# Value products of two batches in one visit, and projection products tilted over eight steps, in a hybrid attention block

## The chip, the cores and the metric

The kernel runs on one core of one Trainium2 chip. Its time is the device time of one execution in microseconds (us); for a kernel with several runs the median is given. Stage times come from one profiled execution.

## The reference, cut to what matters

One layer of an encoder block over 1024 tokens of width 1024, in float32:

```python
h = x @ w_in                       # 3328 columns
q_a, k_a, v_a, z_a, q_b, k_b, v_b, z_b = split(h)
y_a = neighborhood_attention(q_a, k_a, v_a, rel_bias)   # 8 heads of 64, grid 16 x 64, window 8 x 16
y_b = windowed_gqa_with_sink(rotary(q_b), rotary(k_b), v_b, sink)   # 8 query heads, 2 kv heads, |i - j| <= 128
mixed = concat(y_a * silu(z_a), y_b * silu(z_b))
x = layer_norm(alpha * x + mixed @ w_out)
```

Both attentions take a softmax over their scores: `softmax(q k^T / 8 + bias)` in the neighbourhood group (a), and with one more logit for each head, the sink, in the windowed group (b).

## The kernel before, in words

Float32 products are made of float16 parts: each operand is split into a high and a low half, and three products (high x high, low x high, high x low) are summed in PSUM.

**Stages.** A first stage makes the values v of all tokens and the first six of 21 projections (`project`, names in `ORDER`, 48 products of 512 columns each: two halves of 24). The middle stage, which the change touches, runs the attention in *steps*, one for each *unit*. The last stage multiplies by w_out, adds the residual and normalises.

**Units, batches and quads.** A unit is one head's softmax for 128 queries. There are 128: 64 of group b, then 64 of group a. Four units in a row form a *batch* for the scores and a *quad* q for the values; quad q is units 4q to 4q+3, and its scores are batch q. Quads 0 to 15 are of group b, 16 to 31 of group a.

**What happens to a unit.** The scores of a batch go to four of five PSUM banks named `s` (`batch`, `stage_mm`, L933). DVE adds the bias and takes the row's extreme (`stage_qk`, L958, tiles `sn` and `nm`), ACT takes the exponential and its sum (`stage_exp`, L974), DVE the reciprocal of the sums of two units (`stage_sum`, L980 and L981, tile `ri`). Then `stage_tr` splits the probabilities into halves (ACT L992, DVE L993, tile `split`), which empties the bank, and SP issues a transposing DMA to tile `tr` (L999), of which three quads' worth exist. The value products of a quad (`stage_pv`, L1035) read `tr` and the values (`vb` or, gathered by `gather_v`, `va`) and write one half of the only bank `t`: even quads the first half, odd quads the second. `stage_z` (L1043 and L1046, DVE) multiplies that half into the gate tile `z`, which frees it.

**Steps.** In the loop over steps i, every fourth step (i = 3, 7, 11, ...) issues the scores of the next batch, and behind them the value products that `PV_AT` has for this step: quad q at step 4q + 11, with the last two at 131 and 135. `Z_AT` gives the step of the z product, mostly 4q + 13.

**Projections as filling.** The other 15 projections and the first products with w_out (60 of them, L1165) run between these on TensorE. They form the list `fill`; `pump_to(u)` issues as many of them as are due by the time u, which may lie within a step. `FILL_AT` has the steps at which each projection begins, `WARP` bends the time within four steps. A finished half of a projection is taken out of its PSUM bank `pj` (two banks) by `evac`: by ACT and DVE, for rotary ones by POOL too. Such operations wait in queues of the program for each engine (`enq`), from which `pop(engine, n, top)` emits those that are due at fixed places of a step; `top` = 0 takes only the urgent ones, such as the emptying of a `pj` bank. `need` emits one at once, where something depends on it.

**Order.** The order of each engine's instructions is the order of emission, fixed when the program is built. Nothing overtakes on an engine or in SP's queue of DMA issues.

Of the kernel before, what the change touches and what calls it, by code (L numbers as in the profile page):

```python
# [25 lines left out]
QSCALE = 2.0 ** -15  # L26
BH, BR, NX, F1 = 6, 6, 6, 0.2
NSPLIT, NP = 6, 2
ORDER = ["zb0", "z0", "zb1", "kb", "qb0", "z1", "qb1", "zb2", "qb2", "k0", "qb3", "q0", "zb3", "k1", "q1",
         "k2", "q2", "k3", "q3", "z2", "z3"]  # L30
NPRO = 6
NS = 21 - NPRO
ZPRO = (0, 1, 2, 5)
ZSUM = (1, 6, 13, 14)
DSUM = (4, 7)
SUMS = list(range(11)) + [13, 11, 14, 12]
NR = 8
# [1 line left out]
SCALE_AT = ((4, 6), (7, 2))  # L39
K_ORDER = (5, 0, 6, 1, 7, 2, 3, 4)  # L40
FILL = ORDER[NPRO:]
FILL_AT = [0, 8, 17, 25, 33, 41, 49, 57, 65.5, 74, 82, 90, 98, 106, 113.5, 122.5, 125, 127, 128.5, 131.5, 136]
ZTAG = {"z3": "zv", "zb3": "zc", "z2": "zs", "zb1": "zd", "zb2": "ze"}
X2POOL = (1, 3, 5)
WVPOOL = (3, 5)
# [5 lines left out]
WO_PRE = (9, 10, 12, 13, 14, 15)  # L51
WO_POST = (7, 8)
WO_MAX = 88
EO = (4, 5, 6, 7, 0, 1, 2, 3)
LAST = ((0, 384), (384, 128))
NPE = 384
# [18 lines left out]
def hybrid_block(ctx, tc, xT, x, wt, wv, wo, bias, sink, gain, lbias, cos, sin, bmask, out):  # L75
# [45 lines left out]
    invt = const.tile([128, 2], F32, name="invt")  # L121
    NT = len(ORDER)
    xsc = const.tile([128, 1], F32, name="xsc")
# [56 lines left out]
    def pop(eng, n, top=1, late=0):  # L180
        q = queues[eng]
        ready = [op for op in q if op.prio <= top and all(
            d.step is not None and d.step + d.lag < clock["step"] + late for d in op.deps)]
        ready = sorted(ready, key=lambda op: op.prio)[:n]
        for op in ready:
            q.remove(op)
            op.emit()
        return len(ready)
# [7 lines left out]

    NH = 2 * len(ORDER)
    NL = NH - 2 * NR
# [54 lines left out]
    def w_scale(n, tag="s"):  # L253
# [14 lines left out]
        nc.vector.tensor_scalar(v, v, xrs, 0.5, op0=ALU.mult, op1=ALU.mult)  # L268
        nk, nq = ORDER.index("kb"), ORDER.index("qb0")
        if n >= NPRO - 1:  # L270
# [165 lines left out]
    with ExitStack() as vctx:  # L436
# [180 lines left out]
        for k in range(KT):  # L617
# [6 lines left out]
            for ps in FIRST if k == 0 else SECOND if k == 1 else ([(t, a, i) for i in range(3)] for t, a in T1):  # L624
# [5 lines left out]
                if k > 1:  # L630
                    g = T1.index((t, a))
# [369 lines left out]
    def quad(q):  # L1001
        g, p, j, t = units[4 * q]
        return g, p, t // 2 if g == "b" else t[0]
# [52 lines left out]
    def pump_to(u):  # L1056
        n = 0
        k = int(u) % 4
        u = int(u) // 4 * 4 + 4 * (WARP[k] + (WARP[k + 1] - WARP[k]) * (u - int(u)))
        for k, c in enumerate(FILL_N):  # L1060
            u0, u1 = FILL_AT[k], FILL_AT[k + 1]
            n += int(c * min(max((u - u0) / (u1 - u0), 0), 1))
        pump(n - pumped[0])
        pumped[0] = max(n, pumped[0])
# [89 lines left out]
    NU = len(units)  # L1154
# [163 lines left out]
                need(*stk_ops[u[1], 0], *stk_ops[u[1], 1])  # L1318
        stage_mm(us)

    PV_AT = {4 * q + 11: q for q in range(30)}
    PV_AT.update({131: 30, 135: 31})
    Z_AT = {4 * q + 13: q for q in range(30) if q not in (24, 25, 28, 29)}
    Z_AT.update({115: 24, 116: 25, 127: 28, 129: 29, 132: 30, 136: 31})

    clock["step"] = 0
    scan_ops = []
    for i in range(-LD, NU + LO):
# [44 lines left out]
            stage_z(Z_AT.pop(i))  # L1373
        if i > Z3_END:
            pop("dve", 1, 0)
        if i % 4 == 1 and i < NU:
            for u in units[i - 1:i + 1]:
                stage_tr(u)
# [2 lines left out]
                stage_tr(u)  # L1381
        if i in Z_AT:
            stage_z(Z_AT.pop(i))
        early = pop("act", 1, 0)
        if i in M_SCALE:
            m_scale(M_SCALE.index(i))
        if WO_MAX + 4 <= i < WO_MAX + 7:
            wo_scale(i - WO_MAX - 4)
        pump_to(i + F1)
        if i - 1 in PV_AT and quad(PV_AT[i - 1])[0] == "a":  # L1390
            _, p, b = quad(PV_AT[i - 1])
            if p < 3:
                gather_v(p + 1, b)
        free = 2 if i % 4 > 1 or i >= NU else 0
        turned = pop("dve", free if i < 105 else 1 + free)
        if i % 4 == 0 and i < NU:
            stage_exp(units[i])
        if i in PV_AT or i % 4 == 3 and i + 1 < NU:
            if i < NU:
                stage_sum(units[i - 1:i + 1])  # L1400
            pump_to(i + QK_AT)
            if i + 1 < NU:
                batch(i + 1)
            if i in PV_AT:
                stage_pv(PV_AT[i])
            if i + 1 < NU:
                stage_qk(units[i + 1])
        pop("act", max(free + (1 if free and (i >= 105 or len(queues["act"]) > 6) else 0) - early, 0))
# [82 lines left out]
```

## Time and profile before

| | |
|---|---|
| median of 3 runs | 442.02 us (441.68 to 442.64) |
| profiled execution | 441.74 us, of it 439.9 us span |
| busy TensorE, DVE, ACT, POOL | 431.4, 345.7, 298.5, 213.2 us |
| middle stage (first scores to last value products) | 122.3 to 362 us |
| projection products, 128x512 f16 (L404) | 1008 |
| score products (L933), value products (L1035) | 384, 720 |

A line of a timeline has the start, the length, engine, line, operation, tile written and tiles read, shape and count, and, in brackets, how long the engine had been idle and what ended that. A line of the waits has who waited for whom, microseconds in total, how many times, and the longest. PE is TensorE's products; their ends are modelled, so the distance of two starts says more than the length of one.

### The profile page before, as it was taken

How to read it: one execution, taken by the hardware profiler on the slowest of the kernel's cores; microseconds unless marked ns; L12 is line 12 of the kernel's file. 1: busy time of each engine (PE TensorE's matmuls, PEld its weight loads, DVE VectorE, ACT ScalarE, POOL GpSimd, SP SyncE). 2: the span in 40 equal slices, each digit the busy share in tenths (PEclk: the TensorE clock that was granted, in tenths of full speed). 3: DMA queues.
4: the chain of work that ended last, by engine and by line, in shares of the span. 5: the costliest groups of instructions: out<-in, count | busy, mean ns of one | idle time of the engine just before them, and what ended most of it. 6: DMA issues, size and time to landing. Idle time of an engine off the chain costs nothing. (4 is left out here: it accounts for less than half of the span.)

```text
span 439.9 us, 8794 instructions
## 1 busy us (share of the span) xinstructions
PE 431.4 (98%) x2955; PEld 232.7 (53%) x2955; DVE 345.7 (79%) x897; ACT 298.5 (68%) x697; POOL 213.2 (48%) x204
## 2 busy tenths in 40 slices
PE   9999999999999999999999999999999999999994
PEld 8987754444443545454545555454545554444442
DVE  5999948729988889888887888888868729089954
ACT  7798259777577888678888999888876756002211
POOL 0205733565944937567505566568452158005840
PEclk9999999999999999999999999999999999999998
DMA  8992078977846869897979999899999978101721
GB/s 299 312 371 66 20 246 263 291 271 250 299 119 145 158 120 190 148 148 157 175 155 203 158 182 219 199 210 190 223 222 207 185 178 330 43 1 72 262 74 72
DMA packets 133981, 81.72 MB, mean 186 GB/s; under 512 B 101296, under 2 KB 113328, under 8 KB 133680
## 3 DMA queue, kind: packets, MB, share of 16 engines
q1 hardware_dynamic: 133504, 80.67, 74.3%
q10 hardware_dynamic: 432, 0.49, 0.4%
q8 instruction: 23, 0.38, 0.4%
q14 instruction: 22, 0.18, 0.2%
HBM read 50.73 MB, written 9.96 MB: 138 GB/s over the span
## 5 line engine op out<-in xcount | busy, mean ns | idle before, releaser
L404 PE MATMUL ps_pj<-xf,wh 128*128 128x512 f16 x672 | 200.6, 379 | 0.0
L404 PE MATMUL ps_pj<-xf,wl 128*128 128x512 f16 x336 | 127.6, 380 | 0.0
L404 PEld LDWEIGHTS <-wh 128*128 128x128 f16 x672 | 65.1, 98 | 75.0 <-issue 0.5
L1165 PEld LDWEIGHTS <-m 128*128 128x128 f16 x408 | 38.7, 98 | 43.7
L974 ACT ACTIVATE ps_s<-sn,nm 128x385 f32<-128x385 f32 (+3 forms) x96 | 52.2, 544 | 12.0 <-DVE nm L958 10.9
L992 ACT ACTIVATE split<-ps_s,ri 128x384 f16<-128x384 f32 (+2 forms) x96 | 48.5, 539 | 17.4 <-ACT ps_s L974 15.4
L993 DVE SCALAR_TENSOR_TENSOR split<-ps_s,ri,split 128x384 f16<-128x384 f32 (+2 forms) x96 | 52.0, 570 | 5.6 <-ACT split L992 4.6
L404 PEld LDWEIGHTS <-wl 128*128 128x128 f16 x336 | 32.8, 98 | 38.9 <-issue 0.6
L1165 PE MATMUL ps_s<-wo,m 128*128 128x512 f16 (+1 forms) x240 | 53.3, 374 | 0.0
L219 POOL TENSOR_SCALAR wr<-wr,wsc 128x512 f32<-128x512 f32 x26 | 23.0, 883 | 50.1 <-ACT wh L214 49.9
L958 DVE CUSTOM_DVE_ANT_0 sn<-ps_s,bm,nsk 128x384 f32<-128x384 f32 (+1 forms) x64 | 39.5, 632 | 0.0
L958 DVE CUSTOM_DVE_ANT_0 sn<-ps_s,bias,sg 128x264 f32<-128x264 f32 (+1 forms) x64 | 33.8, 544 | 5.0 <-PE ps_s L933 3.8
L901 POOL TENSOR_SCALAR bias<-bias,rsg 128x552 f32<-128x552 f32 (+1 forms) x24 | 18.7, 779 | 36.1 <-DMA bias<-in_bias 25.7
L933 PE MATMUL ps_s<-ks,qs 64*128 64x384 f16 (+4 forms) x384 | 34.2, 305 | 1.1 <-DVE nm L958 0.5
L220 POOL TENSOR_TENSOR wl<-wr,wh 128x512 f16<-128x512 f32 x26 | 32.2, 1240 | 2.2
L1222 ACT ACTIVATE sd<-mv,eps 128x1 f32<-128x1 f32 x8 | 2.4, 294 | 41.8 <-DVE mv L1220 39.5
L1264 POOL TENSOR_TENSOR xr<-xr,gb 128x512 f32<-128x512 f32 x7 | 11.2, 1605 | 35.9 <-ACT xr L1261 35.9
L993 DVE SCALAR_TENSOR_TENSOR split<-px,ri,split 128x384 f16<-128x384 f32 (+2 forms) x32 | 25.1, 783 | 3.3 <-ACT split L992 3.3
L933 PEld LDWEIGHTS <-qs 64*128 64x128 f16 x384 | 16.3, 94 | 21.1 <-issue 14.4
L681 PEld LDWEIGHTS <-xf 128*128 128x128 f16 x216 | 21.0, 98 | 8.4 <-DVE xf L535 0.3
L980 DVE TENSOR_SCALAR ps_s<-sm 128x2 f32<-128x2 f32 x64 | 10.3, 160 | 18.8 <-ACT ps_s L974 17.9
L1165 PE MATMUL ps_pj<-wo,m 128*128 128x512 f16 (+1 forms) x120 | 24.2, 347 | 0.0
(213 smaller groups left out, 804.6 us busy)
## 6 DMA issues: line engine op xcount, KB each, us to landing
ws<-in_wt SPq DMA_DIRECT2D x15, 512.0 KB, 5.5
wr<-in_wt SPq DMA_DIRECT2D x26, 256.0 KB, 3.1
bias<-in_bias SPq DMA_DIRECT2D x16, 276.0 KB, 3.2
wor<-in_wo SPq DMA_DIRECT2D x16, 256.0 KB, 3.7
xr<-in_x SPq DMA_DIRECT2D x8, 512.0 KB, 6.5
xraw<-in_xT SPq DMA_DIRECT2D x15, 256.0 KB, 5.3
out<-xr SPq DMA_DIRECT2D x14, 256.0 KB, 2.0
bias<-in_bias SPq DMA_DIRECT2D x8, 368.0 KB, 3.9
```

The costliest lines, as they stand in the source:

```text
L219: nc.gpsimd.tensor_scalar(raw, raw, scale, 1.0, op0=ALU.mult, op1=ALU.mult)
L220: nc.gpsimd.tensor_sub(l, raw, h)
L404: nc.tensor.matmul(ps, a[:, k % 4, :], mv, start=(k == 0 and i == 0), stop=(k == KT - 1 and i == 2))
L681: nc.tensor.matmul(ps[:, :320], lh[t // 4, k][:, 128 * (t % 4):128 * (t % 4) + 128], rh[k][:, 320 * a:320 * a + 320], start=(k == first an ...
L901: op = enq("pool", lambda: nc.gpsimd.tensor_scalar(bv, bv, rsg, -1.0, op0=ALU.mult, op1=ALU.mult), ld, prio=0)
L933: nc.tensor.matmul(st[u, "ps"][:, :m], *parts[i], start=i == 0, stop=i == 2)
L958: nc.vector.tensor_tensor_reduce(sn[:, :m], ps[:, :m], bias_t, sg[:, c:c + 1], init, op0=ALU.add, op1=ALU.min, accum_out=nm)
L974: nc.scalar.activation(pt[:, :m], sn[:, :m], AF.Exp, bias=nm, scale=-1.0, accum_out=sm)
L992: nc.scalar.activation(hl[:, :m, 0, :c], src, AF.Copy, scale=ri)
L993: nc.vector.scalar_tensor_tensor(hl[:, :m, 1, :c], src, ri, hl[:, :m, 0, :c], op0=ALU.mult, op1=ALU.subtract)
L1165: nc.tensor.matmul(ps, lh[:, ts], rh[:, cs], start=(e == EO[0] and i == 0), stop=(e == EO[-1] and i == 2))
L1264: nc.gpsimd.tensor_mul(xr[:, h1], xr[:, h1], gb[:, h1])
```

## The change: what it does

- `PV_AT` now gives the value products of two quads to one step: q and q + 1, q even, at step 4q + 11, behind the scores of every second batch; quads 30 and 31 at step 135. An even quad keeps its step, an odd one comes four steps earlier; quad 29 moves from 127 to 123, quad 30 from 131 to 135.
- `Z_AT` has the two z products one step apart: 4q + 13 and 4q + 14; quads 30 and 31 at 136 and 137.
- `pump_to` adds up to `TILT` = 0.85 steps to the time between steps 8 and 128, rising over four steps and falling over the next four: more products in the four steps without value products, fewer in those with them.
- `FILL_AT` has the first two projections of the stage in 13.4 steps in place of 17, and the others moved accordingly.
- In `ORDER` zb3 and q0 change places (`ZSUM` follows).
- At the first step of each four, ACT takes one urgent operation from its queue ahead of the splits of the probabilities, not behind them.
- `gather_v` follows the two quads of a step. The condition of the step's end lets step 127, which has no value products any more, still make its sums.

```diff
-ORDER = ["zb0", "z0", "zb1", "kb", "qb0", "z1", "qb1", "zb2", "qb2", "k0", "qb3", "q0", "zb3", "k1", "q1",
+ORDER = ["zb0", "z0", "zb1", "kb", "qb0", "z1", "qb1", "zb2", "qb2", "k0", "qb3", "zb3", "q0", "k1", "q1",
          "k2", "q2", "k3", "q3", "z2", "z3"]
...
-ZSUM = (1, 6, 13, 14)
+ZSUM = (1, 5, 13, 14)
...
-FILL_AT = [0, 8, 17, 25, 33, 41, 49, 57, 65.5, 74, 82, 90, 98, 106, 113.5, 122.5, 125, 127, 128.5, 131.5, 136]
+FILL_AT = [0, 6.6, 13.4, 21.4, 29.4, 37.4, 45.4, 53.4, 61.4, 70, 78.8, 87.6, 96.4, 104.6, 112.3, 122, 125, 127, 128.5, 131.5, 136]
...
+TILT = 0.85
...
         u = int(u) // 4 * 4 + 4 * (WARP[k] + (WARP[k + 1] - WARP[k]) * (u - int(u)))
+        if 8 <= u < 128:
+            u += TILT * (1 - abs(2 * (u % 8) / 8 - 1))
...
-    PV_AT = {4 * q + 11: q for q in range(30)}
-    PV_AT.update({131: 30, 135: 31})
-    Z_AT = {4 * q + 13: q for q in range(30) if q not in (24, 25, 28, 29)}
-    Z_AT.update({115: 24, 116: 25, 127: 28, 129: 29, 132: 30, 136: 31})
+    PV_AT = {4 * q + 11: (q, q + 1) for q in range(0, 30, 2)}
+    PV_AT.update({135: (30, 31)})
+    Z_AT = {4 * q + 13 + k: q + k for q in range(0, 30, 2) if q != 24 for k in range(2)}
+    Z_AT.update({114: 24, 115: 25, 136: 30, 137: 31})
...
+        early = pop("act", 1, 0) if i % 4 == 1 else 0
         if i % 4 == 1 and i < NU:
             for u in units[i - 1:i + 1]:
                 stage_tr(u)
...
-        early = pop("act", 1, 0)
+        early = early or pop("act", 1, 0)
...
-        if i - 1 in PV_AT and quad(PV_AT[i - 1])[0] == "a":
-            _, p, b = quad(PV_AT[i - 1])
-            if p < 3:
+        for q in PV_AT.get(i - 1, ()):
+            g, p, b = quad(q)
+            if g == "a" and p < 3:
                 gather_v(p + 1, b)
...
-        if i in PV_AT or i % 4 == 3 and i + 1 < NU:
+        if i in PV_AT or i % 4 == 3 and i < NU:
...
-            if i in PV_AT:
-                stage_pv(PV_AT[i])
+            for q in PV_AT.get(i, ()):
+                stage_pv(q)
```

## The prediction

> **What bounds the kernel now.** I read the page's busy line first, then the same quantities by stage, then the waits of TensorE, then TensorE's own timeline around batches.
>
> ```profile
> span 439.9 us, 8794 instructions
> PE 431.4 (98%) x2955; PEld 232.7 (53%) x2955; DVE 345.7 (79%) x897; ACT 298.5 (68%) x697; POOL 213.2 (48%) x204
> 122.00:150.00 28.00, 26.94 (x170) 12.02 (x168) 23.96 (x74) 23.52 (x59) 15.31 (x15) 1.00 0.63 135
> 150.00:236.00 86.00, 86.00 (x672) 43.66 (x669) 74.48 (x225) 69.56 (x179) 48.41 (x45) 1.00 0.85 160
> 236.00:345.00 109.00, 109.00 (x901) 56.43 (x901) 89.03 (x287) 91.66 (x240) 57.82 (x65) 1.00 1.01 201
> 345.00:362.00 17.00, 16.61 (x152) 9.23 (x151) 7.82 (x23) 11.23 (x26) 6.43 (x7) 1.00 0.84 159
> PE ps_s L933 <- DVE nm L958: 0.5, 1, 0.5
> PE ps_s L933 <- DVE split L993: 0.5, 2, 0.3
> PE ps_t L1035 <- DVE z L1046: 0.4, 1, 0.4
> ```
>
> The windows' columns are the stretch, its length, busy time of PE, weight loads, DVE, ACT and POOL, granted clock (1.00 throughout), DMA share and GB/s. The stage that is changed lies between 122 and 362 us. TensorE is busy in nearly all of it, and its few waits stand at the stage's ends: two batches of scores near 140 and 149 us, one value product near 349. From 150 to 345 us it never waits. So time is won only by giving TensorE less to do, or by removing those waits; and anything that makes it wait is lost in full. DVE (87% in the second window) and ACT (84% in the third) have little room themselves.
>
> But busy is not work. The next rows show TensorE's steps. The number in front is the start; the difference of two starts is what a group occupies.
>
> ```profile
> 401.20 5.18 PE ps_s L1165 x24
> 128.33 1.15 PE L933 MATMUL ps_s<-ks,qs 64*128 64x384 f16 x12
> 129.41 0.39 PE L404 MATMUL ps_pj<-xf,wl 128*128 128x512 f16 x1
> 134.70 1.15 PE L933 MATMUL ps_s<-ks,qs 64*128 64x384 f16 x12
> 140.42 0.33 PE L933 MATMUL ps_s<-ks,qs 64*128 64x384 f16 x1
> 141.26 1.00 PE L933 MATMUL ps_s<-ks,qs 64*128 64x384 f16 x6 [0.51 <-DVE nm L958]
> 142.51 0.48 PE L933 MATMUL ps_s<-ks,qs 64*128 64x256 f16 x5 [0.26 <-DVE split L993]
> 142.93 1.01 PE L1035 MATMUL ps_t<-tr,vb 128*64 128x256 f16 x18
> 148.51 0.81 PE L933 MATMUL ps_s<-ks,qs 64*128 64x256 f16 x7
> 150.10 1.18 PE L1035 MATMUL ps_t<-tr,vb 128*64 128x256 f16 x24
> 156.50 1.15 PE L933 MATMUL ps_s<-ks,qs 64*128 64x384 f16 x12
> 157.58 1.18 PE L1035 MATMUL ps_t<-tr,vb 128*64 128x256 f16 x24
> 158.69 0.39 PE L404 MATMUL ps_pj<-xf,wl 128*128 128x512 f16 x1
> 345.98 3.84 PE L1165 MATMUL ps_pj<-wo,m 128*128 128x512 f16 x17
> 350.21 1.18 PE L1035 MATMUL ps_t<-tr,va 128*64 128x256 f16 x24 [0.39 <-DVE z L1046]
> ```
>
> The first row gives the unbroken pace: 24 products of 512 columns in 5.18 us, 0.216 us each, 0.42 ns a column. By `pump_to`, 24 products lie between the batches at 128.33 and 134.70; from 129.41 to 134.70 is 5.29 us, so 0.11 us is lost where scores (64 rows of the array) follow projections (128 by 128). A batch of scores is six side-by-side pairs of 384 columns, 0.97 us at that pace, and takes 1.08 (128.33 to 129.41): 0.11 us lost where projections follow. A value visit (128 by 64) is six pairs of 256 and six of 128 columns, also 0.97 us, and takes 1.11 (157.58 to 158.69): 0.14 us lost. Every change of the array's shape costs about a tenth of a microsecond, and the profile books it as busy.
>
> **The change, part by part.** *Fewer visits.* Today 32 value visits: 29 behind scores, three by themselves (quads 29, 30, 31 at steps 127, 131, 135). Afterwards 16: fifteen behind scores and one alone. So 14 attached visits and two lone ones go; their products stay. An attached one saves the 0.14 us; a lone one also the 0.11 us of its second switch. That is 14 x 0.14 + 2 x 0.25 = 2.5 us. Some of the 0.14 is pairs of products not starting quite together, which stays; with the 0.11 us of the other two kinds of switch it is 14 x 0.11 + 2 x 0.22 = 2.0. I take 2.1, the plain switch being the cleaner measurement; bounds 1.5 and 2.5. [...]
>
> *First steps fuller.* Worked out from `pump_to`, the products between batches are now 23, 24, 21, 21, then 24 each (23 and 22 around step 60); they become 28, 28, 34, 20, then alternately 29 and 19, later 27 and 18. The batch at 140.42 occupies 2.51 us up to its value products where its 384 and 256 columns need 0.92: 1.6 us lost. The batch at 148.51 occupies 1.59 for the same 0.92: 0.7 us lost. Both wait for DVE to empty PSUM banks. With 22 more products by the fourth batch (22 x 0.216 = 4.8 us) TensorE comes there that much later, more than both waits, and DVE is by then done. What covers this is work taken from later steps: the later batches have fewer products (24, 16, 19, 13 in place of 23, 21, 19, 17). If DVE were just as late, 2.3 us would come back.
>
> *The end.* From 345.98, 17 products (3.67 us) and a switch (0.11) end near 349.76; the value product starts at 350.21. So 0.4 us is lost waiting for the z product of the quad two before, which shares its half of PSUM. Afterwards that z product runs at step 125 or 126 and the value products at step 135, so this wait goes. Together 1.6 + 0.7 + 0.4 = 2.7 us of waits go; nothing below zero can come from their removal, and zero only if each is replaced.
>
> *Odd quads four steps earlier.* This is the price. Quad q's value products need the transposes of its probabilities, which SP issues and which land late:
>
> ```profile
> 200.55 0.99 PE L933 MATMUL ps_s<-ks,qs 64*128 64x384 f16 x12
> 202.53 0.66 DVE L958 CUSTOM_DVE_ANT_0 sn<-ps_s,bm,nsk 128x384 f32<-128x384 f32 x1
> 212.46 2.50 SPq L999 DMA_TRANSPOSE tr<-split  x2
> 316.27 0.88 PE L933 MATMUL ps_s<-ks,qs 64*128 64x264 f16 x12
> 316.93 0.49 DVE L958 CUSTOM_DVE_ANT_0 sn<-ps_s,bias,sg 128x264 f32<-128x264 f32 x1 [0.40 <-PE ps_s L933]
> 327.12 2.58 SPq L999 DMA_TRANSPOSE tr<-split  x2
> DMA to landing us min/median/max: 2.4/3.2/5.0
> DVE ps_s L980 <- ACT ps_s L974: 7.7, 15, 0.8
> DVE sn L958 <- PE ps_s L933: 3.8, 6, 1.1
> ACT split L992 <- ACT ps_s L974: 7.5, 14, 0.8
> ```
>
> (The last three are the waits of DVE from 150 to 236 and from 236 to 345 us, and of ACT from 150 to 236.) In the windowed group, quad 11's last transpose is issued about 213.7 and lands by the median at 216.95: 16.4 us behind the start of its scores. In the neighbourhood group, quad 27's lands at 328.4 + 3.2, 15.3 us behind. Today the value products come three batches behind, near 22 us, with 5 us to spare. Afterwards an odd quad's come two batches behind, second in the pair. In the windowed group that is 0.92 + 1.11 + 0.97 + 19 x 0.216 + 0.11 = 7.2, then 0.92 + 29 x 0.216 + 0.11 = 7.3, then scores and first quad 1.08 + 1.0: 16.6 us. It fits by 0.2. In the neighbourhood group (18 and 27 products) it is 7.0 + 6.9 + 0.9 + 1.1 = 15.9, against 15.3: it fits by 0.6. At two places it doesn't. Quad 15 has the thin steps already and the late landing still: 15.9 against 16.4, 0.5 us. Quad 29 has 16 and 19 products between: 6.7 + 5.25 + 0.8 + 1.1 = 13.9 against 15.3, 1.4 us. Behind a waiting value product stand all further projections, since TensorE runs its products in order. Sum 1.9 us; bounds 0 (landings at the 2.4 us minimum and an earlier chain) and 4.
>
> *The remaining edits.* ACT's copy of a finished projection group moves ahead of the probability splits at the first step of each four. ACT idles there anyway (7.5 us in 14 waits), so I cost it at nothing, and it may free ACT 0.4 us a batch; if the group isn't finished yet, the splits come later by that. Both z products of a pair fall into one batch, 0.4 us on DVE, which waits there for ACT (7.7 us in 15). Two gathers of values go into SP's queue together, ahead of an odd quad's first transposes, not its last. zb3 before q0 changes only which product is pumped when. All at nothing, with the DVE and ACT risk in the second rival.
>
> *Sum* against the profiled execution, 441.74 us (span 439.9): - 2.1 - 2.7 + 1.9 = 438.8. The median of the runs is 0.3 above that execution, so 439.1.
>
> **Rivals.** *No new waits*: the transposes land in time everywhere. For it: 0.2 and 0.6 us to spare, and a chain that may be quicker. Against: quad 29. 441.74 - 4.8 + 0.3 = 437.2.
>
> *DVE and ACT set the pace.* From 150 to 236 us DVE waits only for ACT, never for TensorE: softmax then goes at its own 7.2 us a batch. From 236 to 345 it waits 3.8 us for TensorE, so its own pace is (109 - 3.8)/15 = 7.0. The new steps leave 7.3 and then 6.9. Short by 0.1 over 15 batches: 1.5 us on top, 440.6. For it: 87% and 84% busy; against it: the ACT edit.
>
> *Slower: odd quads' transposes are late in the whole neighbourhood group.* There DVE now starts a batch 0.66 us behind its scores (316.27, 316.93); in the windowed group 1.98 (200.55, 202.53). If that delay lasts, because ACT now stands behind a projection group that ends only after two value visits, every landing moves from 15.3 to 16.6 against 15.9: 0.7 us at each of seven pairs, 4.9, and quad 29 1.3 more than forecast. 438.8 + 6.2 - 0.5 + 0.3 = 444.8 (quad 15's 0.5 is among the seven). It decides from 0.4 us a pair: 4.8 + 0.9 us must be eaten, quad 29 eats 2.7 of it. Against it: a TensorE that waits lets DVE catch up.
>
> *The waits at 140 and 149 us stay* because DVE is later too: 439.1 + 2.3 = 441.4, about no change.
>
> **How the numbers follow.** Forecast 0.52, no new waits 0.12, DVE and ACT 0.19, waits that stay 0.06, slower 0.11. A measurement of this kernel tells about 0.2%, 0.9 us, from no change: faster 0.83, same 0.06, slower 0.11. The range runs from just below the rival without waits, 437.0, to 441.3: it takes in DVE and ACT's pace and the bounds of the waits, and leaves out the slower case and most of the no-change one.
>
> **What would show it.** Right: 16 value groups of 36 to 48 products in TensorE's timeline in place of 32, each closed by a single switch; batches near 140 and 149 us at 0.9 to 1.1 us; no wait on z near 349; the first TensorE waits on transposes at the pairs behind batches 17 and 31. Wrong: waits of value products at most of the 15 pairs (third rival), waits of scores on `split` in the middle (second), or a second quad that costs 1.1 us and not 0.97 although nothing switches before it, which would take away the first term.

## The result, and the profile after

The changed kernel takes 447.65 us (median of 4 runs, 447.17 to 448.57) against 442.24 us for the kernel before (4 runs). The ratio is 1.0126, with a 95% interval from 1.0113 to 1.0138: slower by 5.4 us, where 439.1 was forecast. The profiled execution took 448.57 us, 446.8 of it span.

First the page's busy line and its row of granted clock by slices, then TensorE's stretches (same columns as before), then TensorE's waits over the whole span.

```profile
span 446.8 us, 8768 instructions
PE 434.0 (97%) x2955; PEld 234.6 (53%) x2955; DVE 343.6 (77%) x897; ACT 298.9 (67%) x697; POOL 211.1 (47%) x204
PEclk9999999999999999999999999899999899999999
122.00:150.00 28.00, 28.00 (x193) 13.47 (x192) 22.98 (x71) 22.40 (x56) 15.87 (x16) 1.00 0.63 130
150.00:236.00 86.00, 85.53 (x677) 43.53 (x674) 72.43 (x219) 68.37 (x176) 45.47 (x42) 1.00 0.75 150
236.00:345.00 109.00, 104.65 (x848) 53.54 (x843) 84.99 (x277) 88.39 (x232) 58.03 (x64) 0.98 0.97 195
345.00:369.00 24.00, 22.58 (x178) 12.10 (x176) 13.15 (x41) 17.40 (x41) 8.42 (x10) 0.93 0.95 200
PE ps_t L1036 <- DMA tr<-split: 5.1, 6, 2.0
PE ps_s L934 <- DVE split L994: 1.0, 4, 0.3
```

The first stretch is better than before: no wait, 193 products where there were 170. The loss lies behind 236 us. TensorE is busy for 104.65 us of 109, where it was busy throughout, and two slices of granted clock show 8. The waits name the transposes: six waits, all behind 247 us. TensorE's timeline shows each kind of step, first the good ones, then the bad ones:

```profile
145.05 0.99 PE L934 MATMUL ps_s<-ks,qs 64*128 64x384 f16 x12
145.97 2.00 PE L1036 MATMUL ps_t<-tr,vb 128*64 128x256 f16 x42
147.90 0.60 PE L405 MATMUL ps_pj<-xf,wh 128*128 128x512 f16 x2
152.32 0.99 PE L934 MATMUL ps_s<-ks,qs 64*128 64x256 f16 x12
...
203.30 0.66 PE L934 MATMUL ps_s<-ks,qs 64*128 64x384 f16 x6
204.17 0.27 PE L934 MATMUL ps_s<-ks,qs 64*128 64x256 f16 x1 [0.21 <-DVE split L994]
204.69 0.48 PE L934 MATMUL ps_s<-ks,qs 64*128 64x256 f16 x5 [0.26 <-DVE split L994]
...
276.49 1.11 PE L934 MATMUL ps_s<-ks,qs 64*128 64x352 f16 x12
277.53 1.18 PE L1036 MATMUL ps_t<-tr,va 128*64 128x256 f16 x24
280.66 1.39 PE L1036 MATMUL ps_t<-tr,va 96*64 96x256 f16 x24 [1.95 <-DMA tr<-split]
281.99 0.61 PE L405 MATMUL ps_pj<-xf,wl 128*128 128x512 f16 x1
282.39 1.06 PE L405 MATMUL ps_pj<-xf,wh 128*128 128x512 f16 x2
...
284.93 0.59 PE L405 MATMUL ps_pj<-xf,wh 128*128 128x512 f16 x2
```

At 145.05 and 152.32 the batches that waited before run without a break (twelve products in one row, 0.92 us from 145.05 to 145.97), and 42 value products of two quads take 1.93 us in one visit. At 203.30 a new wait of the scores stands. At 277.53 the even quad's products run, and the odd quad's (quad 19) start at 280.66, 3.13 us later instead of 1.01. Behind that wait the projection products start 0.42 to 0.43 us apart (282.39 to 283.25 for two) and not 0.216: the array runs at half its clock for seven products, until 284.93 (granted clock 0.50 from 281.48 to 284.90 us).

I made an account of the middle stage: from each distance of two starts on TensorE the time that its columns need is taken, and 0.095 us where the array's shape changes (from 150 to 345 us of the kernel before each kind of change takes 0.090 to 0.098 at the median); what is left over, where it is more than 0.045 us, is a wait.

| us | before | after |
|---|---|---|
| first scores to last value product | 239.5 | 246.8 |
| waits near 140 and 149; for z at 349 | 1.9; 0.5 | 0; 0 |
| waits of odd quads' value products for transposes | 0 | 6.1 |
| half clock behind them | 0 | 3.1 |
| other waits of scores (203, 349) | 0 | 2.0 |
| the stage without waits | 237.2 | 235.6 |
| what follows the stage | 78.1 | 77.8 |

So the products did get cheaper by 1.6 us and the old waits are gone. 11 us of new ones outweigh both. The odd quads that wait are 15, 17, 19, 27 and 29 (1.4, 0.95, 2.1, 0.7 and 0.9 us). For them, and for quad 23, which doesn't wait, the next table has the issue and the landing of the quad's last transpose, in us behind the start of its scores, and the time until TensorE stood ready for its value products:

| quad | before: issued, landed | after: issued, landed | ready |
|---|---|---|---|
| 15 | 12.1, 17.1 | 14.1, 17.1 | 15.6 |
| 17 | 12.1, 14.8 | 13.2, 18.0 | 17.0 |
| 19 | 12.6, 15.6 | 13.7, 18.5 | 16.4 |
| 23 | 11.9, 15.3 | 12.1, 15.4 | 16.1 |
| 27 | 12.1, 15.8 | 12.8, 16.1 | 15.4 |
| 29 | 12.5, 15.4 | 13.9, 16.7 | 15.8 |

The split of a quad's last probabilities, which this transpose waits for, tells where the issue was delayed. For quads 15, 19 and 27 the split was done within 0.3 us of its time before (11.2, 10.5 and 10.1 us behind the scores before, 11.1, 10.7 and 9.8 after), but the issue came 1.0 to 2.1 us later behind it: that is SP's queue. For quads 17 and 29 the split itself came 1.1 and 2.1 us later, and the queue took no longer.

The landings themselves, for SP's transposes from 236 to 345 us, of the kernel before (one row), then of the kernel after, then for the two last ones of quad 19 (274.4 to 276 us), then SP's queue behind 260 us, and what the DMA engines carried from 236 to 345 us (packets, MB, share of 16 engines; KB each and median us to landing):

```profile
DMA to landing us min/median/max: 2.8/3.5/5.0
L1000 SPq DMA_TRANSPOSE tr<-split x59: 1188/1227/3145, 235.1 to 342.7; - x59
DMA to landing us min/median/max: 2.7/3.4/5.5
L1000 SPq DMA_TRANSPOSE tr<-split x2: 1217/1218/1219, 274.5 to 275.8; - x2
DMA to landing us min/median/max: 4.8/5.1/5.3
266.47 2.54 SPq L1000 DMA_TRANSPOSE tr<-split  x2
269.06 1.09 SPq L851 DMA_DIRECT2D va<-vwin  x2
270.26 0.45 SPq L898 DMA_DIRECT2D bias<-in_bias  x1
270.84 2.60 SPq L1000 DMA_TRANSPOSE tr<-split  x2
273.48 0.58 SPq L898 DMA_DIRECT2D bias<-in_bias  x1
274.48 6.19 SPq L1000 DMA_TRANSPOSE tr<-split  x4
q1 hardware_dynamic: 55088, 21.09, 96.7%
bias<-in_bias SPq DMA_DIRECT2D x13, 276.0 KB, 3.3
tr<-split SPq DMA_TRANSPOSE x59, 3.4
```

A transpose takes 1.23 us of SP's queue, and the queue has hardly a gap: from 266.47 each issue starts within 0.6 us of the end of the one before. The packets fill 96.7% of the DMA engines' time. Landing then takes anything from 2.7 to 5.5 us, and quad 19 met both of its last two at 4.8 and more. Yet as a whole the landings are those of the kernel before, 3.5 us at the median and 5.0 at the longest; there every quad had a batch to spare.

### The profile page after: what moved, and what is told of

Read it like the earlier page. It is cut to its first block, busy times and chain, and to the rows that moved or that the text cites. A ratio compares the mean times of both kernels' runs of the same rounds, so it can differ in the third digit from the quotient of the medians.

```text
span 446.8 us, 8768 instructions
## 1 busy us (share of the span) xinstructions
PE 434.0 (97%) x2955; PEld 234.6 (53%) x2955; DVE 343.6 (77%) x897; ACT 298.9 (67%) x697; POOL 211.1 (47%) x204
## 5 line engine op out<-in xcount | busy, mean ns | idle before, releaser
L405 PE MATMUL ps_pj<-xf,wh 128*128 128x512 f16 x672 | 203.6, 381 | 0.0
L994 DVE SCALAR_TENSOR_TENSOR split<-ps_s,ri,split 128x384 f16<-128x384 f32 (+2 forms) x96 | 52.0, 570 | 13.0 <-ACT split L993 12.6
L1267 POOL TENSOR_TENSOR xr<-xr,gb 128x512 f32<-128x512 f32 x7 | 11.2, 1606 | 40.0 <-ACT xr L1264 40.0
L994 DVE SCALAR_TENSOR_TENSOR split<-px,ri,split 128x384 f16<-128x384 f32 (+2 forms) x32 | 24.1, 753 | 1.6 <-ACT split L993 1.5
```

The costliest lines, as they stand in the source:

```text
L405: nc.tensor.matmul(ps, a[:, k % 4, :], mv, start=(k == 0 and i == 0), stop=(k == KT - 1 and i == 2))
L994: nc.vector.scalar_tensor_tensor(hl[:, :m, 1, :c], src, ri, hl[:, :m, 0, :c], op0=ALU.mult, op1=ALU.subtract)
L1267: nc.gpsimd.tensor_mul(xr[:, h1], xr[:, h1], gb[:, h1])
```

## The experiments

Theories: **A**, the odd quads' transposes come too late for the earlier visits, and little else matters. **B**, DVE and ACT set the pace, so that what TensorE saves comes back as waits. For what makes the transposes late: **D**, SP's queue of issues is full; **E**, they are slow on the way, behind the loads' bytes and other packets. Each run is compared with the kernel before on the same chip; "stage" and "waits" are of the account above, from one profiled execution each.

**Odd quads without a transpose to wait for** (const_odd: kernel after; in `stage_pv`):

```diff
...
+                    if q % 2:
+                        mv = fixed[:c, 0:len(blocks), :]
...
```

> The changed kernel, but the value products of the odd quads read a constant tile in place of their transposed probabilities (left out: the odd quads' real probabilities in the value products; the transposes are still made). Instructions, sizes and order on TensorE stay; only the wait of each odd quad for its transposes is gone. Theory A, the odd quads' transposes land too late: the 7.5 us of waits at the pairs behind batches 17, 19, 21, 29 and 31, and the 2 us at half clock behind the longest of them, go, and about 1 us of waits of scores stays: 438 to 439.5 us, ratio to before 0.992. Theory B, DVE and ACT set the pace once the later steps have fewer projection products: TensorE then waits at the scores in place of the value products, and the time stays at 444 or more. Theory C, the gate projection zb3 holds ACT up behind POOL's rotary products and everything late comes from that: 446 to 447.

Measured: 442.72 us, 1.0015 [1.0000, 1.0030]. TensorE's waits and DVE's from 236 to 345 us:

```profile
PE ps_s L936 <- DVE split L996: 1.3, 5, 0.3
DVE sn L961 <- POOL bias L904: 1.6, 2, 1.4
```

Taking this one wait away brings 4.9 of the 5.4 us: A holds for the loss. But the time is no better than before, and 3 us above what A forecast. The stage takes 239.8 us, of which 4.4 are waits, 3.8 of them of scores for DVE, and DVE waits for the bias, a load that POOL scales. About half of these waits of scores, near 204 and 346 us, stood in the kernel after too; those near 289 and 297 us are new. So something on DVE's side stands right behind A. Whether that is the softmax's pace as a whole (B) or single late pieces, this run doesn't tell.

**No pairs** (single: kernel after with `PV_AT` and `Z_AT` of before, `TILT` = 0, all else as after):

> The changed kernel with one quad at a visit again (steps of the value and z products as before, no tilt); the fuller first steps, zb3 before q0 and ACT's earlier urgent operation stay. Theory A: no wait for transposes, since they have 5 us again; the 2.3 us of waits at 140 and 149 us are gone; the switches are not saved: 439.5 to 441, ratio 0.996. Theory B: thinner later steps alone slow it: scores wait from 240 us on, 442 to 445. Theory C: a wait of ACT for POOL of 1 to 2.5 us near 200 us and with it a wait of scores of up to 1 us: 441 to 442.

Measured: 442.94 us, 1.0019 [1.0004, 1.0035]; stage 239.7, waits 2.75.

```profile
PE ps_t L1036 <- DVE z L1047: 1.9, 1, 1.9
```

The waits at the start are gone here too, and nothing is won: they come back at 343 and 349 us, the latter on z, where 0.5 us stood before. So the waits for transposes go, as A says, but the time is 2 us above its forecast. The wait of scores behind the thinned steps, near the stage's end, stands in every run with the new or late2's `FILL_AT`, 0.7 to 1.6 us long (0.2 in step12), and in none of the kernel before, pair_only, before_light and before_actq, which have the old one. The first steps' gain is in part paid back there. These runs don't part `FILL_AT` from ACT's earlier operation, which came with it.

**Pairs alone** (pair_only: kernel before with the pairs and the tilt; `FILL_AT`, `ORDER` and ACT's place as before):

> The kernel before with the pairs and the tilt alone: the old places of the projections (FILL_AT, ORDER) and the old place of ACT's urgent operation. If the pairs' early odd quads cost the time (A), they wait here too, 4 us or more in all at quads 15 to 29, and the time is 446 to 449, with the two waits of the scores near 140 and 149 us back. If the fuller first steps cause the waits, because later steps get fewer products, the odd quads wait 2 us or less and the time is 440 to 442.

Measured: 444.98 us (442.93 to 447.12), 1.0067 [1.0044, 1.0090]. In the profiled execution value products wait 4.3 us, at quads 13, 15, 19 and 29; the last is

```profile
346.08 1.18 PE L1036 MATMUL ps_t<-tr,va 96*64 96x256 f16 x24
349.24 1.18 PE L1036 MATMUL ps_t<-tr,va 128*64 128x256 f16 x24 [1.97 <-DMA tr<-split]
```

The time is between the two expectations: pairing and tilting alone cost about half of the loss, and the other edits add to it. The waits of scores near 142 and 150 us are back, as expected, 1.4 us.

**zb3 behind k1 and q0** (after_ord2: kernel after with `ORDER` ... "qb3", "k1", "q0", "zb3", ... and `ZSUM`, `DSUM` to match):

> The changed kernel with k1, q0 and zb3 in this order behind qb3, so that the gate zb3, which takes over the tile of the cosines, comes 16 steps behind the last rotary projection and not directly behind it. Theory C: without ACT's 2.4 us wait near 200 us the wait of the scores there goes (0.9 us) and what follows is earlier by as much; were it the root of the late transposes, 440 us. Theory A: only the 0.9 us go, the waits at the odd quads of the second half stay: 446 to 447, ratio 1.010.

Measured: 445.49 us, 1.0082 [1.0054, 1.0110]; the wait at 203 us is gone, the five odd quads still wait, 5.7 us. The wait of quad 19 is 2.0 us as in the kernel after, but no half clock follows it (granted clock 0.999 over the profiled execution, 0.991 in the kernel after). Why the wait was there shows in ACT's waits of the kernel after, from 150 to 236 us:

```profile
ACT z L365 <- POOL rp_raw L337: 2.4, 1, 2.4
```

With zb3 straight behind qb3 its Tanh takes the tile that qb3's rotary product on POOL still uses; ACT waits 2.4 us, with the splits of the probabilities behind it, and the scores wait for these. In `single`, with this order but neither pairs nor tilt, no such wait of scores appears: it takes both the order and these.

**Landing time** (step12): each pair one step later, by itself in the middle of the projection products (`PV_AT` 4q + 12, `Z_AT` 4q + 14 and 15).

> The kernel after with each pair of quads one step later, by itself at step 4q + 12 in the middle of the projection products, its z products one step later too. Each odd quad has some 1.7 us more to land, and each of 15 pairs has one more change of the array's shape, 0.11 us. The kernel after's waits at the pairs are 0.9 to 2.5 us long. If landing time is all that was missing (A), 1.5 us of waits or less stay of 6.7 and no half clock behind them; the time is 447.6 - 5.2 - 2.3 + 1.7 = 441.8, 441 to 443.5. If the softmax runs late as a whole (B), the waits come back in the scores, and the time is 444 or more.

Measured: 446.98 us (median of nine executions, 443.42 to 449.62), 1.0115 [1.0086, 1.0145]; value products wait 5.0 us, at quads 19, 27 and 29 alone.

```profile
347.99 1.18 PE L1036 MATMUL ps_t<-tr,va 96*64 96x256 f16 x24
351.64 0.77 PE L1036 MATMUL ps_t<-tr,va 128*64 128x256 f16 x5 [2.47 <-DMA tr<-split]
```

A failed here in the form that 1.7 us are missing. Quads 15 and 17 are cured, but quad 29's last transpose was issued 15.3 us behind its scores and landed at 18.9; quad 19's took 5.8 us. The lateness isn't a fixed amount: quad 29's last transpose had been issued 13.9 us behind its scores in the kernel after. Four steps later it is nearly gone, at another price:

**Pairs four steps later** (late2: an odd quad three batches behind again, an even one four; with the ORDER above):

```diff
-BH, BR, NX, F1 = 6, 6, 6, 0.2
+BH, BR, NX, F1 = 8, 5, 6, 0.2
...
-    PV_AT = {4 * q + 11: (q, q + 1) for q in range(0, 30, 2)}
+    PV_AT = {4 * q + 15: (q, q + 1) for q in range(0, 30, 2)}
...
-TILT = 0.85
+TILT = -0.85
...
```

> Two quads at a visit, but at step 4q + 15 and not 4q + 11: the odd quad keeps its step of before, the even one comes four steps later. For this there are eight tiles of transposed probabilities in place of six, and five bias tiles in place of six; the tilt is turned round; k1, q0, zb3 in this order. Theory A: every quad has 5 us or more between landing and use, so no wait for transposes, the switches are saved (2.1 us) and the waits near 140 and 149 us too: 437 to 439.5 us, ratio 0.992. Theory B: the pace of DVE and ACT shows as waits of scores instead: 443 or more. If five bias tiles are too few, DVE waits for POOL's bias products more than 3 us in the second half.

Measured: 441.67 us, 0.9994 [0.9981, 1.0007]: no difference, and not A's 437 to 439.5. (`FILL_AT` and `Z_AT` are moved to match. The profiled execution took 443.05 us, so its waits are on the high side.) Value products wait 0.7 us, the stage without its waits is 235.7, as short as in the kernel after. But it takes 240.9, since waits of 5.2 us came back, 3.0 of them of scores. DVE's waits from 236 to 345 us:

```profile
DVE ps_s L981 <- ACT ps_s L975: 10.1, 18, 1.4
DVE split L994 <- ACT split L993: 6.0, 20, 1.4
DVE sn L959 <- POOL bias L902: 3.4, 4, 1.4
```

In the kernel before DVE waited 3.8 us here for scores; now no such row is there, and the bias is late instead. TensorE has overtaken the softmax: B.

**A lighter softmax** (const_light, after_light, before_light: half of DVE's low halves of the probabilities left out, in the kernels const_odd, after and before):

```diff
-        nc.vector.scalar_tensor_tensor(hl[:, :m, 1, :c], src, ri, hl[:, :m, 0, :c],
+        nc.vector.scalar_tensor_tensor(hl[:, :m, 1, :c // 2], src[:, :, :c // 2], ri, hl[:, :m, 0, :c // 2],
```

> The kernel whose odd quads read a constant tile, and besides DVE makes only half of each low half of the probabilities (left out: the odd quads' probabilities in the value products, and the second half of the low parts). That takes some 30 us off DVE's 187 us in the stage, and changes nothing for TensorE. Theory B, the softmax chain of DVE and ACT is a second bound of the stage, at 239.6 us, whatever TensorE saves: its 4.4 us of waits of scores go and the stage comes down to TensorE's own 235.4 us: 438 to 438.5 us, ratio 0.991. Theory C, the waits come from single late pieces (POOL's rotary products, bias loads and POOL's bias products): 441 to 442.

> The changed kernel, where DVE makes only half of each low half of the probabilities (left out: the second half of the low parts). The odd quads wait for their real transposes. Theory A, the transposing DMAs and SP's queue make the odd quads late: their waits stay at 4 us or more, 443 to 445. Theory B, the softmax chain makes them late: DVE is up to 1 us earlier in each batch, the waits shrink to under 2 us: 438.5 to 440.5.

> The kernel before, where DVE makes only half of each low half of the probabilities (left out: the second half of the low parts). Theory B: the 2.4 us of waits near 140, 149 and 349 us go, no others come, TensorE's own 237.2 us remain: 439.5 to 440, ratio 0.995. With the constant odd quads on the same light DVE it measures what the saved switches are worth alone: 1.6 to 2 us. If TensorE alone bounded the kernel before, apart from DVE's delay at the start, the same.

Measured: 444.34 us, 1.0055 [1.0034, 1.0076]; 447.45, 1.0123 [1.0091, 1.0156]; 441.93, 0.9994 [0.9979, 1.0010]. The kernel after keeps its 5.6 us of value waits: the softmax's load isn't what makes most of the transposes late. The edit took 17 us off DVE in the stage (195.3 to 178.1 us from 122 to 362 us), not 30. The stage does get shorter, 237.7 in place of 239.8 without odd quads' waits and 238.7 in place of 239.5 in the kernel before. That is about half of what B forecast for the first and a third for the last: 2.3 us of waits stay in const_light, and most of the waits near 140 and 148 us stay in before_light. So DVE's load is a part of the second bound, and what the rest is stays open. And even this gain doesn't arrive, as the waits of the first of these kernels show:

```profile
PE ps_s L1172 <- POOL wo L1141: 2.9, 1, 2.9
```

The last stage's products wait for POOL's low half of w_out, which in const_light and before_light (1.3 us there) comes late: a third bound. The profiled execution of const_light took 442.55 us, its median is 1.8 us higher, and no trace shows why.

**Work moved from ACT and DVE to POOL** (late2_m: late2 with the high halves of m and two low halves of w_out on POOL):

> Two quads at a visit at step 4q + 15 with eight tiles of transposed probabilities, as before, and besides POOL in place of ACT makes the high halves of the first four mixed tiles (8 copies of 0.6 us), and POOL in place of DVE two low halves of w_out (2 of 0.7 us). All of the reference's work is done. Theory B: the chain is shorter by up to 5 us of ACT's work and 1.5 of DVE's, of which a part lies in the chain: 439.5 to 441, 1 to 2 us below the same kernel without it. Theory A, waits are set by DMA and queue: no change, 441.5.

Measured: 444.12 us, 1.0049 [1.0034, 1.0064]. The stage falls to 237.4, 3.5 less than in late2 (whose profiled execution was 1.4 us above its median), so work of ACT and DVE was what held most of it, as B says. The time was forecast 439.5 to 441 and isn't reached: behind the stage TensorE waits 2.8 us for POOL's w_out and then loses 1.7 us to half clock (granted clock 0.994 over the profiled execution, 0.998 in late2).

**Fewer, larger loads** (after_merge: one bias load for two heads), and the same in late2 (late2_merge):

> The changed kernel, but the bias tiles of both heads of a pair come in one load, not two (three double tiles in place of six single ones, the same bytes): 12 issues fewer on SP's queue, some 0.6 us each, nothing else. From 236 to 345 us SP's issues alone fill 98 of 109 us in the kernel before, 61 transposes of 1.22 us and more among them. Theory D, SP's queue of issues is what makes the odd quads' transposes late, and bias loads too: with 7 us less to issue the waits for transposes fall from 6.7 to under 3 us: 442.5 to 444.5. Theory E, the transposes are late on their way (DMA engines), not in the queue: the waits stay over 5 us, 446 to 448.

> Two quads at a visit at step 4q + 15 with eight tiles of transposed probabilities and k1, q0, zb3 in this order, now with one bias load for two heads (two double tiles in place of five single ones). Theory D: SP's queue, 98% full in its second half, gets 7 us of room, and the 3 us of waits of scores there shrink: 440 to 441. If two double tiles are too few, DVE waits for bias products instead: 442 or more.

Measured: 453.7 us, 1.0243 [1.0202, 1.0284], and 442.99, 1.0001 [0.9985, 1.0017]. From 236 to 345 us the loads and transposes of the first stand so:

```profile
bias<-in_bias SPq DMA_DIRECT2D x6, 552.0 KB, 4.7
bias<-in_bias SPq DMA_DIRECT2D x4, 736.0 KB, 6.9
tr<-split SPq DMA_TRANSPOSE x56, 4.2
```

Half as many issues of loads, and the transposes land 0.8 us later at the median (the longest 7.3 us), though SP's queue now has gaps of up to 4.6 us; value products wait 11 us. D alone falls: room in the queue didn't shorten the waits, and with the same bytes in larger pieces the landings got longer. In late2_merge DVE's wait for the bias is down to 0.3 us, but waits of scores of more than 3 us stay. So neither SP's queue nor the bias alone holds late2; this too speaks for B.

**The bias loads from ACT's queue** (after_actq, before_actq: `nc.sync.dma_start` to `nc.scalar.dma_start`), in the kernel after and the kernel before:

> The kernel after, with the neighbourhood group's bias loads issued by ACT in place of SP. Their number and size stay; SP's queue gets free of 12.2 of the 98 us that it spends on issues between 236 and 345 us. If the odd quads' transposes are late because SP's queue is full (D), the value products' waits (6.7 us in the kernel after) fall to 2 us or less where the group's waits are (quads 17, 19, 27, 29), and the time to 442 to 444, unless ACT's issues slow the softmax. If they are late on the way (E: the loads' bytes and the instruction packets, wherever the loads were issued), 4.5 us or more of these waits stay and the time stays at 446 to 449.

> The kernel before with the same edit, the bias loads issued by ACT. It says what the edit itself costs or brings: if ACT has the room, 441 to 442; if the issues lengthen ACT's chain, waits of the scores come between 236 and 345 us and the time is 443 or more. The edit's effect on the kernel after is read against this one.

Measured: 445.25 us, 1.0081 [1.0050, 1.0112], and 442.88, 1.0020 [0.9995, 1.0045]. From 236 to 345 us in the kernel after with this edit:

```profile
bias<-in_bias ACTq DMA_DIRECT2D x14, 276.0 KB, 3.3
tr<-split SPq DMA_TRANSPOSE x61, 4.1
```

2.4 us better than the kernel after, but the profiled execution has no half clock (granted clock 0.998 over it, 0.991 in the kernel after), and as after_ord2 shows, that can go without the waits. The queue had a share: the last transposes of quads 15, 19 and 29 were issued 3.0, 3.0 and 2.1 us behind their split in the kernel after, and 0.9 us here. But 5.2 us of value waits stay, now at other quads (17 and 21 above all), and the transposes' landing goes from 3.4 to 4.1 us (to 4.0 in before_actq, where hardly anything waits for it): what they gain in SP's queue they lose on the way. So neither D nor E holds alone. before_actq, at 442.88 between its two expectations, says that the edit itself brings nothing.

**More issues in the kernel before** (before_sp: 24 loads of 4 KB added to SP's queue):

> The kernel before with one more load of 8 columns for each of its 24 bias loads, into a tile that nobody reads: 24 issues of 0.4 to 0.6 us more on SP's queue, almost no bytes. Theory D, SP's queue is as good as full in the second half: 98 + 12 us of issues no longer fit into 109, and the time grows by 3 to 10 us. Otherwise the 5 us that every quad has in this kernel swallow it: less than 1 us.

Measured: 453.48 us, 1.0237 [1.0212, 1.0262].

```profile
DVE sn L960 <- POOL bias L903: 13.9, 7, 3.7
PE ps_t L1037 <- DVE z L1048: 5.3, 2, 4.1
```

SP's queue had no room in the kernel before either: the last transpose of quad 29 is issued 6.4 us behind its split, in place of 2.8, while the landings get no longer (3.2 us at the median). The bias suffers first: DVE waits 13.9 us for it, and its loads stand in the same queue. In the kernel before none of it was seen, because every late landing had a spare batch.

**TensorE's instructions shifted** (phase: kernel after with 72 products of the first stage cut in two): TensorE's own instructions come by 16 KB packets, 23 in the kernel after, a median of 254 of its products and weight loads apart and 15.8 us between 140 and 360 us, and from 276 to 279 us of the kernel after one stands among quad 19's transposes:

```profile
q1 hardware_dynamic: 814, 0.36, 136.0%
q8 instruction: 1, 0.02, 3.4%
```

> The changed kernel, where two projections of the first stage (kb and qb0) have 72 of their products cut into two of 256 columns: 72 products and 72 weight loads more, at no cost in columns. TensorE's instructions, of which 256 come in each 16 KB packet of instructions, are thereby shifted by 144, more than half a packet, some 8 us in the middle stage. Theory F, transposes that are under way stand still for 1 to 2 us while such a packet comes, and odd quads wait where that falls on their last transposes: the waits move to other quads than 15, 17, 19, 27 and 29, and their sum changes. Theory D: the same quads wait, for about the same time, 447 to 448.5.

Measured: 450.2 us (448.21 to 452.64), 1.0172 [1.0128, 1.0217]. That is above the 447 to 448.5 of D. In the kernel after, packets had come at 241.62, 260.70 and 276.63 us, on the transposes of quads 15, 17 and 19, and none on those of 27 and 29. With the packets elsewhere quad 17 no longer waits (0.95 us before), quad 11 does (1.3 us at 221.83, a packet at 221.00), and 15, 19, 27 and 29 still do, though no packet falls on the transposes of 15 and 19 now. The waits of value products sum to 7.3 us. So, by one profiled execution, such a packet helps decide which quad waits, and quads wait without one too.

**Two attempts at a faster version** (single_end, pair_b2): no pairs but the last, z of quad 28 at step 125; and that with pairs up to quad 13, where the DMA engines have room (share 0.75 from 150 to 236 us of the kernel after, 0.97 from 236 to 345).

> The kernel after with single visits at steps 4q + 11 for quads 0 to 29 and one pair, 30 and 31, at step 135; no tilt; the z products at 4q + 13 again, so that z of quad 28 runs at step 125 as in the kernel after. The run `single` had one wait of 1.9 us left, of quad 30's value product on that z. If the time is set by TensorE's waits, it goes: 442.9 - 1.9 - 0.2 = 440.8, a ratio of 0.997. If a second bound stands behind it (softmax, the loads, or POOL's low halves of w_out at the start of the last stage), a wait of about that size comes elsewhere and the time stays at 442 to 443.

> The kernel single_end with pairs for quads 0 to 13 alone, where the DMA engines have room (0.75 to 0.85 busy from 150 to 236 us against 1.0 from 236 on) and where the kernel after had no late odd quad; the tilt up to step 64 alone, and zb3 behind k1 and q0, which took the wait near 203 us away. If the pairs are bad only for the landing (A), the seven visits fewer bring 7 x 0.11 to 7 x 0.14, 0.8 to 1.0 us, over single_end: 440.0, no value product waits 0.5 us or more before quad 30. If the softmax sets the pace (B), scores wait later for as long as was saved, and the time is that of single_end within 0.5 us.

Measured: 441.93 us, 0.9995 [0.9986, 1.0004], and 444.11, 1.0037 [1.0019, 1.0055]. The wait on z stayed in both (1.6 us), and the seven visits saved came back: waits of scores for `split` at 259 and 294 us, 1.7 us, in the profiled execution of the second. That execution took 442.34 us; the median is 1.8 us higher, which no trace explains. No version was found that beats the kernel before by more than a measurement tells.

## Why the prediction was wrong

**Fewer visits** was right: forecast 2.1 us, measured 1.6 (237.2 - 235.6) for 18 changes of shape fewer, 0.09 each. A pair of quads takes 1.93 where two single visits took 0.95 + 1.11 = 2.06, and only one switch ends it.

**First steps fuller** and **The end** were right in themselves: the waits near 140, 149 and 350 us are gone, 2.4 us of the 2.7 forecast. What was wrong was to count them as gone for good. With the odd quads' waits removed, or with single visits, waits of 2 to 4 us on DVE stand later, so this gain had nowhere to go. That is nearest to the second rival, which was priced at 1.5 us and given 0.19; const_odd puts all such waits at 4.4, and a lighter DVE takes away about half of them. One term of this step was put at nothing and wasn't: the work taken from the later steps. Behind the thinned steps scores wait 1.3 us in the kernel after, near 350 us, where nothing waited for DVE's splits before.

**Odd quads four steps earlier** is the step that failed. It was sized 1.9 us; it measured 6.1 us of waits and 3.1 us of half clock behind them. The room was sized well: 15.9 us forecast for quads 15 to 27 of group a, 15.4 to 17.0 measured; for quad 29 13.9 and 15.8, which is luck: 1.3 us of it is the new wait of scores just ahead. The landing was not. It was worked out for one quad of each group, with the issue time of before (13.2 and 12.1 us behind the scores) and the median landing of 3.2 us, to be compared with margins of 0.2 and 0.6 us. That median was of the whole kernel; from 236 to 345 us it was 3.5. The row that was quoted beside it said 2.4 to 5.0, and the table above shows that already before quads 15 and 27 landed at 17.1 and 15.8, too late for the new visits with nothing else changed. A median says that half of the landings are later. From 269.06 to 274.48 us SP's queue had gaps of at most 0.42 us: what stood ahead of quad 19's first transposes could hold up its last ones too. So the two gathers together, put at nothing, weren't nothing: 1.09 us at 269.06, ahead of quad 19's. How much of its later issue they are, no run parts. Two loads on the same path were also in view and unused: the DMA share of 1.01 in the quoted window, and SP's unbroken queue. The issue moved, by up to 2 us; the landings as a whole did not, but quads 17 and 19 met long ones (4.8 us and more) without a spare batch. Quad 29 was expected to be the worst and was one of five. The third rival had the outcome, a loss at many pairs, but not the cause: it had every landing of the group later because DVE starts later, and the splits of quads 15, 19 and 27 were at most 0.2 us later. Its 444.8 us was still too low, for the half clock was in no case.

**The remaining edits** were put at nothing. With the pairs and the tilt, zb3 before q0 costs the wait of 0.8 us at 203: it does change more than which product is pumped when, because two projections next to each other share a tile. What ACT's earlier urgent operation does alone wasn't tried.

Of what would have shown the steps right, the 16 groups, the batches at 145 and 152 us and the visits without an inner switch came as written. The first waits were expected behind batches 17 and 31, and did stand there; that they also stood behind 19, 21 and 29 is the failed step.

What stays open: what makes up the rest of the second bound beside DVE's load, how much of the lateness the loads' bytes and how much the queue would cause alone, and why single runs of the paired kernels lie up to 6.2 us apart (443.42 to 449.62 for the pairs one step later). A stretch of half clock, which comes behind a wait or doesn't, may be a part of that (the granted clock of these nine runs is 0.988 to 0.999).

## What to carry to other kernels

Merging visits on the busiest engine moves a consumer earlier; weigh the new slack against the latest landings that the trace shows, one by one, and not against their median, above all where the DMA share is near 1 (here 0.97 to 1.01 from 236 to 345 us) and the issuing queue has hardly a gap. When several stages are all near their limit, a wait that is removed is worth only the distance to the next bound: find that bound first, with a kernel that leaves the suspected wait out altogether. And a wait can cost more than its length: quad 19's 2.1 us were followed by 3.4 us at half clock.

## What the runs showed of the hardware

- Behind one wait of about 2 us TensorE ran at half clock, behind others it didn't. In the kernel after, quad 19's wait of 1.95 us (2.1 by the distance of starts) was followed by products 0.427 us apart in place of 0.216, for 3.4 us (the row below). The wait of 1.97 us in the pairs alone (granted clock 0.998 over the profiled execution) and the longest of 2.3 us in the kernel with ACT's loads (1.00 from 236 to 345 us) had none behind them.

```profile
281.48:284.90 3.42, 3.42 (x20) 1.38 (x16) 3.17 (x11) 2.90 (x9) 3.00 (x3) 0.50 0.64 125
```

- In the kernel after the granted clock changed at whole multiples of 3.413 us: full clock lasted 276.48, 68.27 and 88.75 us, which is 81, 20 and 26 such steps, and the two half clocks between lasted one step each. In the kernel before it changed first after 433.49 us, 127 of them. Both half clocks came right behind the steps with the most idle time of TensorE between 118 and 432 us, summed from the timeline: 1.95 us before 281.48 (the wait that ends at 280.66) and 1.35 us before 353.16 (those that end at 350.25, 350.77 and 353.17). No other step there held more than 1.1 us, and none was followed by half clock. In the kernel before none held more than 0.9, and there the clock stayed full. How much idle time it takes, these two traces don't show.
- Transposes that met a 16 KB packet of instructions landed later. Around 276.6 us the transposes' packets took up to 1.5 us each, and quad 19's landed after 4.8 to 5.3 us. In the kernel after, between 150 and 360 us, the 26 transposes that met such a packet in their first 2.7 us landed after 4.2 us at the median, the 88 others after 2.9; in the kernel before it was 4.3 and 3.2.
- Small loads were not cheap in a full queue. In before_sp an issue of 4 KB takes 0.38 us of SP's queue at the median, one of a bias tile 0.57; 24 of the small ones, 9 us of issuing, made the kernel 11 us slower.

```profile
L899 SPq DMA_DIRECT2D spare<-in_bias x24: 328/382/1427, 229.8 to 353.2; - x24
L898 SPq DMA_DIRECT2D bias<-in_bias x24: 454/570/578, 229.2 to 352.5; - x24
```
